# Six weight slots, a shared tile for the final norm's weights, and another order of pairs in a decoder trunk

## The chip, the cores and the metric

The kernel runs on one core of one Trainium2 chip. The metric is the device time of one execution in microseconds, as the median of several runs. Before the change it is 2187.33 us, the median of 3 runs from 2186.57 to 2188.96.

## What is computed

A two-layer decoder over 256 positions and 2048 channels, all in float32. Layer 0 mixes with a sliding-window attention beside an mLSTM, layer 1 with a forgetting attention; every layer is followed by a gated feed-forward part, and a norm ends the trunk:

```python
def swiglu(xn, w_gate, w_up, w_down):
    return (jax.nn.silu(xn @ w_gate) * (xn @ w_up)) @ w_down

    for layer in range(DEPTH):
        ...
        h = h + mix.astype(h.dtype)
        h = h + swiglu(rms_norm(h, norm_ffn[layer]), w_gate[layer], w_up[layer], w_down[layer])
    return rms_norm(h, norm_final)
```

The hidden width of the gated part is 5632. The weights, some 400 MB in all, are read once.

## The kernel before

**Three products for one.** To keep float32 precision with fast matmuls, every operand is split in two rounded parts, `hi` and `lo`, and a product is the sum of three matmuls: hi by hi, hi by lo, lo by hi (L164 to L166 in the projections, L345 to L347 in the gated part). Activations are split once (`xh`, `xl`, `mh`, `ml`). Weights are split as they stream in. `load_raw` (L85) has SyncE (SP) issue the load of a raw tile of 2 x 128 rows by 512 columns, 512 KB; the pool `wr` holds four such tiles. `split_chunk` (L138) lets ScalarE (ACT) round it to `hi` (L141) and VectorE (DVE) subtract to get `lo` (L142). The pool `wp` holds the `hi` and `lo` tiles, four slots of each. A raw slot comes free when VectorE has read it, a hi or lo slot when TensorE (PE) is through with it.

**The gated part.** `ffn` (L416) goes through the 11 groups of 512 hidden columns in two parts of 6 and 5 groups (`HALVES`). After the groups of a part comes a down projection over that part (L444 to L456). `gate_up` (L352) makes one group: it takes the 16 row blocks as 8 pairs, in the order of `ORDER` (L34), whose entries are (mixed or not, pair). For a plain pair it loads and splits one gate tile and one up tile and issues 2 x 2 x 2 x 3 = 24 matmuls. For a mixed pair, three of the eight, it computes the 2 x 2 block product of two row blocks of activations with gate and up with seven block products instead of eight, 21 matmuls. For that VectorE forms four combinations of the raw weights in the tile `t4` (L378 to L381; one buffer of 8 KB per partition), which are split in turn into `ht` and `lt` (L389, with the line of the helper L240 and L241 in the profile; two buffers each), and `lo` of one half tile (L384, also L241). The combinations of activations, `sh` and `sl`, come from `sums_of` (L199) while the output projection of the mixer writes its columns; `MIXED` names the pairs that have them. After the eight pairs VectorE adds the partial products up in the tile `c` (L405 to L413), ScalarE applies silu, VectorE multiplies (L430), and TensorE transposes `c` (L438) for the down projection.

**The end.** `finish` (L818) is called for each of the four column blocks of the last down projection. It adds to the residual `h`, squares, and multiplies by the final norm's weights `gf` (L827, for the last block L837). `gf` is 2048 floats on each of 128 partitions, 8 KB per partition, 1 MB to write. It has a tile of its own and is loaded by a DMA that GpSimd (POOL) issues (L813). Nothing precedes that load in its dependences, so it goes out at the start of the kernel. The power in L834 runs on POOL.

**The start.** SP loads the four column pieces of x and the first weights alternately (L96 to L99). TensorE transposes x piece by piece (L219) and multiplies with the key weights.

**Who orders the work.** The source is written in program order, and the Tile scheduler orders each engine's queue anew by a simulated timeline; within a queue an engine then works strictly in order. The number of slots and the order of pairs thus decide where an instruction stands in its queue.

**The scratch.** Some of each partition of the on-chip memory is set aside for the descriptors of POOL's DMAs. The program is made without a size for it, which gives 16 KB.

Of the kernel before, what the change touches and what calls it, by code (L numbers as in the profile page):

```python
# [7 lines left out]
F32 = mybir.dt.float32  # L8
# [7 lines left out]
P = 128  # L16
D = 2048
# [13 lines left out]
OFF_QM, OFF_KM, OFF_VM, OFF_OM = 1536, 2048, 2560, 3584  # L31
CAP = 15.0
FILL = 24
ORDER = ((0, 0), (0, 4), (1, 1), (0, 5), (1, 2), (0, 6), (1, 3), (0, 7))  # L34
MIXED = [p for w, p in ORDER if w]
HALVES = (0, 6, 11)

# [2 lines left out]
def trunk(  # L40
# [20 lines left out]
    nc = tc.nc  # L61
# [3 lines left out]
    xl = sp_.tile([P, KT, S], F32R, name="xl")  # L65
    mh = sp_.tile([P, KT, S], F32R, name="mh")
    ml = sp_.tile([P, KT, S], F32R, name="ml")
    wp = ctx.enter_context(tc.tile_pool(name="wp", bufs=4))
    wr = ctx.enter_context(tc.tile_pool(name="wr", bufs=4))
    cp = ctx.enter_context(tc.tile_pool(name="cp", bufs=1))  # L70
    sm = ctx.enter_context(tc.tile_pool(name="sm", bufs=2))
# [75 lines left out]
    def new_acc():  # L147
        return [pa.tile([P, NB], F32, tag="acc", name="acc") for _ in range(NT)]

    def gemm(acc, lhs, w, c0, n, k_from, k_to, k_all, skew=1):  # L150
        k0 = k_from
        while k0 < k_to:
            last = k_to == k_all and k0 + skew * CK >= k_all
            chunks = [load_chunk(w, kc, c0, n) for kc in range(k0, k_all if last else k0 + CK, CK)]
            order = [(i, t) for i in range(len(chunks) * CK) for t in range(NT)]
            if last:
                order.sort(key=lambda it: it[1])
            for i, t in order:
                k = k0 + i
                hi, lo = (c[:, i % CK, 0:n] for c in chunks[i // CK])  # L160
                ah, al = lhs(k)
                ts = slice(t * P, (t + 1) * P)
                o = acc[t][:, 0:n]
                nc.tensor.matmul(o, ah[:, ts], hi, start=(k == 0), stop=False)  # L164
                nc.tensor.matmul(o, ah[:, ts], lo, start=False, stop=False)  # L165
                nc.tensor.matmul(o, al[:, ts], hi, start=False, stop=(k == k_all - 1))  # L166
            k0 += len(chunks) * CK
# [4 lines left out]
    def m_of(k):  # L172
        return mh[:, k, :], ml[:, k, :]

    def project(w, c0, n):
        acc = new_acc()
        gemm(acc, x_of, w, c0, n, 0, KT, KT)
        return acc
# [3 lines left out]
    def square_sum(key, n):  # L182
        if n == 0:
            sums[key] = sm.tile([P, NT, 4], F32, tag="ss", name="ss")
        for t in range(NT):
            junk = sm.tile([P, NB], F32, tag="junk", name="junk")
            nc.scalar.activation(
                junk, h[:, t, n * NB : (n + 1) * NB], AF.Square, accum_out=sums[key][:, t, n : n + 1]
            )

    def rstd(key):
        tot = sm.tile([P, NT], F32, tag="tot", name="tot")
        nc.vector.reduce_sum(tot, sums[key], axis=AX)
        nc.vector.tensor_scalar(tot, tot, 1.0 / D, EPS, op0=ALU.mult, op1=ALU.add)
        r = sm.tile([P, NT], F32, tag="r", name="r")
        nc.gpsimd.tensor_tensor(out=r, in0=tot, in1=mhalf[:, 0:NT], op=ALU.pow)
        return r
# [41 lines left out]
    def split_plain(dst_h, dst_l, src):  # L239
        nc.scalar.copy(dst_h, src)  # L240
        nc.vector.tensor_tensor(out=dst_l, in0=src, in1=dst_h.bitcast(F32), op=ALU.subtract)  # L241

    def add_out(acc, n):
        for t in range(NT):
            o = h[:, t, n * NB : (n + 1) * NB]
            nc.vector.tensor_tensor(out=o, in0=acc[t], in1=o, op=ALU.add)
# [102 lines left out]
    def bank(par, name):  # L349
        return pm.tile([P, NB], F32, tag="pm", name=name) if par else pa.tile([P, NB], F32, tag="acc", name=name)  # L350

    def gate_up(fp, sh, sl, layer, g, par):  # L352
        c0 = g * NB
        plain = [[bank(par, "acc") for _ in range(NT)] for _ in range(2)]
        mixed = None
        count = [s_[0] for s_ in ORDER]
        for pos, (w, pair) in enumerate(ORDER):
            k0 = 2 * pair
            if not w:
                for m, wt in enumerate((w_gate[layer], w_up[layer])):  # L360
                    hi, lo = load_chunk(wt, k0, c0, NB)
                    for i in range(CK):
                        ah, al = x_of(k0 + i)
                        for t in range(NT):
                            ts = slice(t * P, (t + 1) * P)
                            three(
                                plain[m][t], ah[:, ts], al[:, ts], hi[:, i, :], lo[:, i, :],
                                pos == 0 and i == 0, pos == len(ORDER) - 1 and i == CK - 1,
                            )
# [46 lines left out]
    def ffn(layer, fp, sh, sl, eh, el, key, idx_next=None, key_next=None, finish=None):  # L416
        def a_of(k):
            return m_of(k) if k < KT else (eh[:, k - KT, :], el[:, k - KT, :])

        r = rstd(key)  # L420
        for part in range(2):
            g0, g1 = HALVES[part : part + 2]
            nk = 4 * (g1 - g0)
            for g in range(g0, g1):
                par = (g - g0 + part) % 2
                c = gate_up(fp, sh, sl, layer, g, par)
                for t in range(NT):
                    nc.scalar.activation(c[:, t, :], c[:, t, :], AF.Silu, scale=r[:, t : t + 1])
                for t in range(NT):
                    nc.vector.scalar_tensor_tensor(  # L430
                        out=c[:, t, :], in0=c[:, 2 + t, :], scalar=r[:, t : t + 1], in1=c[:, t, :], op0=ALU.mult, op1=ALU.mult
                    )
                for half in range(2):
                    pt = bank(par, "pf").rearrange("p (i q) -> p i q", i=2)
                    for i in range(2):
                        cs = (2 * half + i) * P
                        for t in range(NT):
                            nc.tensor.transpose(pt[:, i, t * P : (t + 1) * P], c[:, t, cs : cs + P], ident)  # L438
                    k = 4 * (g - g0) + 2 * half
                    if k < KT:  # L440
                        split_plain(mh[:, k : k + 2, :], ml[:, k : k + 2, :], pt)
                    else:
                        split_plain(eh[:, k - KT : k - KT + 2, :], el[:, k - KT : k - KT + 2, :], pt)
            wd = w_down[layer][4 * g0 * P : 4 * g1 * P, :]  # L444
            for n in range(4):
                acc = new_acc()
                end = part == 1 and idx_next is None and n == 3
                gemm(acc, a_of, wd, n * NB, NB, 0, nk, nk, skew=3 if end else 1)
                if part == 0:
                    add_out(acc, n)  # L450
                elif idx_next is None:
                    finish(acc, n)
                else:
                    add_out(acc, n)
                    split_scaled(idx_next, n)
                    square_sum(key_next, n)  # L456
# [20 lines left out]
    with tc.tile_pool(name="ev", bufs=1) as ev:  # L477
# [84 lines left out]
        acc = project(wi, OFF_OM + 768, 256 + 8)  # L562
# [53 lines left out]
        with tc.tile_pool(name="mp", bufs=1) as mp:  # L616
# [99 lines left out]
            for g in range(2):  # L716
                acc = project(wi, OFF_VM + g * NB, NB)
# [14 lines left out]
    with tc.tile_pool(name="od", bufs=1) as od:  # L732
# [8 lines left out]
        acc = project(wi1, c_v + 14 * FD, VT + FOX_H)  # L741
# [67 lines left out]
            )  # L809


    gf = cp.tile([P, D], F32, name="gf")
    nc.gpsimd.dma_start(gf, norm_final.partition_broadcast(P))  # L813
    ov = out[0].rearrange("(t p) d -> p t d", p=P)
    fs = cp.tile([P, NT, 4], F32, name="fs")
    ft = cp.tile([P, 3, NT], F32, name="ft")

    def finish(acc, n):  # L818
        ns = slice(n * NB, (n + 1) * NB)
        for t in range(NT):  # L820
            o = h[:, t, ns]
            nc.vector.tensor_tensor(out=o, in0=acc[t], in1=o, op=ALU.add)
            junk = sm.tile([P, NB], F32, tag="junk", name="junk")
            nc.scalar.activation(junk, o, AF.Square, accum_out=fs[:, t, n : n + 1])
            part, mean, rs = (ft[:, a, t : t + 1] for a in range(3))
            if n < 3:
                nc.vector.tensor_tensor(out=o, in0=o, in1=gf[:, ns], op=ALU.mult)  # L827
            if n == 2:
                nc.vector.reduce_sum(part, fs[:, t, 0:3], axis=AX)
                nc.vector.tensor_scalar(part, part, 1.0 / D, EPS, op0=ALU.mult, op1=ALU.add)  # L830
            if n < 3:
                continue
            nc.vector.tensor_scalar(mean, fs[:, t, 3:4], 1.0 / D, part, op0=ALU.mult, op1=ALU.add)
            nc.gpsimd.tensor_tensor(out=rs, in0=mean, in1=mhalf[:, 0:1], op=ALU.pow)  # L834
            nc.scalar.mul(h[:, t, 0 : 2 * NB], h[:, t, 0 : 2 * NB], rs)
            nc.vector.tensor_scalar(h[:, t, 2 * NB : 3 * NB], h[:, t, 2 * NB : 3 * NB], rs, None, op0=ALU.mult)
            nc.vector.scalar_tensor_tensor(out=o, in0=o, scalar=rs, in1=gf[:, ns], op0=ALU.mult, op1=ALU.mult)  # L837
            for half in (1, 0):
                hs = slice(half * 2 * NB, (half + 1) * 2 * NB)
                nc.sync.dma_start(ov[:, t, hs], h[:, t, hs])  # L840

    close_layer(1, w_out_odd[0], 3, "f1", finish=finish)


# [43 lines left out]
```

## Time and profile before

| | us |
|---|---|
| median of 3 runs | 2187.33 |
| lowest, highest | 2186.57, 2188.96 |
| the profiled execution | 2189.5 |
| its span in the profile | 2187.8 |
| matmuls busy in it | 2158.8 |
| VectorE busy | 1526.2 |
| ScalarE busy | 1118.1 |

The profile is of one execution. Its time is 1.7 us longer than the span from the first instruction to the last. Rows of a timeline name the start in microseconds from the start of the span, the busy time, the engine, the line, and out<-in by the names in the program; brackets at the end hold the idle time of the engine before it and who ended it. Rows of stretches show the busy time of each engine with the number of its instructions, the granted clock, the DMA share and GB/s. PEld is the loading of the stationary operand, which overlaps with matmuls. "q0" is the DMA queue of POOL, "q1" that of SP.

### The profile page before, as it was taken

To read this page: it belongs to the slowest core of one execution; us is meant where nothing else is said; L and a number is where in the kernel's file an instruction comes from. 1 tells how busy PE (TensorE), PEld (TensorE's weight loads), DVE (VectorE), ACT (ScalarE), POOL (GpSimd) and SP (SyncE) were. 2 spreads that over 40 slices of the span, in tenths; PEclk is the share of its full clock that TensorE was granted. 3 is DMA by queue.
4 is the path that set the end of the run, shared out by engine and by line. 5 is a ranking of instruction groups with operands and counts; after the bars stand their busy time and mean duration, and the time that the engine had idled before them with its cause. 6 is when DMAs were issued, how large, how long until landed. Compare 5 with 4: busy or idle time off the path is not lost.

```text
span 2187.8 us, 26662 instructions
## 1 busy us (share of the span) xinstructions
PE 2158.8 (99%) x9986; PEld 1782.2 (81%) x9986; DVE 1526.2 (70%) x1874; ACT 1118.1 (51%) x1447; POOL 37.6 (2%) x61
## 2 busy tenths in 40 slices
PE   8999999999999999999999999999999999999998
PEld 6878888877788888888888888888877888888886
DVE  5565567888874688885555555678888844888954
ACT  5565455555543455554545444555555533555543
POOL 2110000000000000000000000000000000000000
PEclk9999999999999999999999999999999999999999
DMA  8544556655666666565675565556565666666564
GB/s 257 149 148 148 171 167 185 198 178 189 202 196 193 191 200 204 174 212 185 182 224 168 169 175 156 181 182 194 190 203 173 212 193 193 195 200 200 189 198 144
DMA packets 213538, 408.34 MB, mean 187 GB/s; under 512 B 12736, under 2 KB 21024, under 8 KB 213152
## 3 DMA queue, kind: packets, MB, share of 16 engines
q1 hardware_dynamic: 212736, 402.90, 59.4%
q0 software_dynamic: 624, 3.72, 0.5%
q8 instruction: 78, 1.28, 0.2%
q14 instruction: 52, 0.43, 0.1%
q10 hardware_dynamic: 48, 0.02, 0.0%
HBM read 404.48 MB, written 2.11 MB: 186 GB/s over the span
## 4 chain that ended last, share of the span: by engine, by line
PE 65%; DVE 16%; DMA 13%; ACT 3%; issue 3%; SPq 0%; DVEq 0%; ACTq 0%; POOLq 0%; POOL 0%
PE acc L164 17%; PE acc L165 17%; PE acc L166 17%; DMA raw<-in_w_up_dram 9%; DVE lo L142 6%; DMA raw<-in_w_gate_dram 3%; PE acc L346 3%; PE acc L347 3%; PE acc L345 3%; DVE lt L241 2%; ACT hi L141 2%; DVE c L413 2%; DVE t L380 1%; DVE t L378 1%; PE prod L345 1%
## 5 line engine op out<-in xcount | busy, mean ns | idle before, releaser
L142 DVE TENSOR_TENSOR lo<-raw,hi 128x1024 fp32r<-128x1024 f32 (+3 forms) x710 | 851.2, 1202 | 490.2 <-ACT hi L141 488.1
L141 ACT CAST hi<-raw 128x1024 fp32r<-128x1024 f32 (+3 forms) x710 | 731.5, 1033 | 785.9 <-PE acc L166 498.0
L346 PE MATMUL acc<-lo,xh 128*128 128x512 f32 x946 | 369.9, 391 | 4.4 <-DVE lo L142 4.3
L347 PE MATMUL acc<-hi,xl 128*128 128x512 f32 x946 | 366.2, 390 | 0.0
L345 PE MATMUL acc<-hi,xh 128*128 128x512 f32 x946 | 349.8, 390 | 0.3 <-DVE c L407 0.3
L164 PE MATMUL acc<-hi,mh 128*128 128x512 f32 x768 | 299.9, 392 | 1.2 <-ACT mh L240 1.2
L165 PE MATMUL acc<-lo,mh 128*128 128x512 f32 x768 | 300.7, 392 | 0.0
L166 PE MATMUL acc<-hi,ml 128*128 128x512 f32 x768 | 298.4, 390 | 0.0
L165 PE MATMUL acc<-lo,xh 128*128 128x512 f32 (+3 forms) x736 | 276.0, 375 | 0.4 <-DVE lo L142 0.4
L164 PE MATMUL acc<-hi,xh 128*128 128x512 f32 (+3 forms) x736 | 275.1, 378 | 1.2 <-ACT hi L141 1.2
L166 PE MATMUL acc<-hi,xl 128*128 128x512 f32 (+3 forms) x736 | 276.2, 376 | 0.0
L346 PEld LDWEIGHTS acc<-lo,xh 128*128 128x128 f32 x946 | 177.6, 188 | 43.5 <-DVE lo L142 7.3
L345 PEld LDWEIGHTS acc<-hi,xh 128*128 128x128 f32 x946 | 177.6, 188 | 38.3 <-DVE c L407 0.8
L347 PEld LDWEIGHTS acc<-hi,xl 128*128 128x128 f32 x946 | 177.7, 188 | 36.3
L240 ACT CAST ht<-t 128x1024 fp32r<-128x1024 f32 x132 | 137.3, 1052 | 120.9 <-DVE t L381 59.4
L164 PEld LDWEIGHTS acc<-hi,mh 128*128 128x128 f32 x768 | 144.2, 188 | 31.2 <-ACT mh L240 1.4
L166 PEld LDWEIGHTS acc<-hi,ml 128*128 128x128 f32 x768 | 144.2, 188 | 29.6
L165 PEld LDWEIGHTS acc<-lo,mh 128*128 128x128 f32 x768 | 144.2, 188 | 29.2
L241 DVE TENSOR_TENSOR lt<-t,ht 128x1024 fp32r<-128x1024 f32 x132 | 158.2, 1217 | 2.9 <-ACT ht L240 2.7
L164 PEld LDWEIGHTS acc<-hi,xh 128*128 128x128 f32 x736 | 138.3, 189 | 26.4 <-issue 2.0
L165 PEld LDWEIGHTS acc<-lo,xh 128*128 128x128 f32 x736 | 139.1, 189 | 24.7 <-DVE lo L142 1.1
L166 PEld LDWEIGHTS acc<-hi,xl 128*128 128x128 f32 x736 | 139.1, 189 | 23.9 <-issue 0.3
(273 smaller groups left out, 2222.1 us busy)
## 6 DMA issues: line engine op xcount, KB each, us to landing
raw<-in_w_gate_dram SPq DMA_DIRECT2D x176, 512.0 KB, 4.0
raw<-in_w_up_dram SPq DMA_DIRECT2D x176, 512.0 KB, 4.6
raw<-in_w_down_dram SPq DMA_DIRECT2D x176, 512.0 KB, 3.7
raw<-in_w_in_odd_dram SPq DMA_DIRECT2D x88, 512.0 KB, 3.8
raw<-in_w_in_even_dram SPq DMA_DIRECT2D x64, 512.0 KB, 3.8
raw<-in_w_out_even_dram SPq DMA_DIRECT2D x32, 512.0 KB, 3.7
raw<-in_w_out_odd_dram SPq DMA_DIRECT2D x32, 512.0 KB, 3.7
raw<-in_w_in_odd_dram SPq DMA_DIRECT2D x8, 272.0 KB, 2.8
```

Source lines behind the costliest of these rows:

```text
L141: nc.scalar.copy(hi[:, :, 0:n], raw[:, :, 0:n])
L142: nc.vector.tensor_tensor(out=lo[:, :, 0:n], in0=raw[:, :, 0:n], in1=hi[:, :, 0:n].bitcast(F32), op=ALU.subtract)
L164: nc.tensor.matmul(o, ah[:, ts], hi, start=(k == 0), stop=False)
L165: nc.tensor.matmul(o, ah[:, ts], lo, start=False, stop=False)
L166: nc.tensor.matmul(o, al[:, ts], hi, start=False, stop=(k == k_all - 1))
L240: nc.scalar.copy(dst_h, src)
L241: nc.vector.tensor_tensor(out=dst_l, in0=src, in1=dst_h.bitcast(F32), op=ALU.subtract)
L345: nc.tensor.matmul(o, ah, hi, start=start, stop=False)
L346: nc.tensor.matmul(o, ah, lo, start=False, stop=False)
L347: nc.tensor.matmul(o, al, hi, start=False, stop=stop)
L378: nc.vector.tensor_tensor(out=t4[:, 0, :], in0=ru[:, 0, :], in1=rg[:, 0, :], op=ALU.subtract)
L413: nc.vector.tensor_tensor(out=o, in0=plain[m][t], in1=o, op=ALU.add)
```

## The change

The hi and lo pool gets six slots of each instead of four, 16 KB more per partition. To make room, `gf` loses its own tile: its load is written after the groups of the last part, into the buffer of `t4` (same tag, one buffer), whose last contents are read by then; and the DMA scratch is given 8 KB instead of 16. The order of pairs becomes 0 1 2 4 3 5 6 7, with 2, 3 and 6 mixed, where it was 0 4 1 5 2 6 3 7 with 1, 2 and 3 mixed. The pattern of plain and mixed places is the same.

```diff
-ORDER = ((0, 0), (0, 4), (1, 1), (0, 5), (1, 2), (0, 6), (1, 3), (0, 7))
+ORDER = ((0, 0), (0, 1), (1, 2), (0, 4), (1, 3), (0, 5), (1, 6), (0, 7))
...
-    wp = ctx.enter_context(tc.tile_pool(name="wp", bufs=4))
+    wp = ctx.enter_context(tc.tile_pool(name="wp", bufs=6))
...
+            gf = None
+            if part == 1 and finish is not None:
+                gf = fp.tile([P, D], F32, tag="t4", name="gf", bufs=1)
+                nc.gpsimd.dma_start(gf, norm_final.partition_broadcast(P))
             wd = w_down[layer][4 * g0 * P : 4 * g1 * P, :]
             for n in range(4):
                 acc = new_acc()
...
-                    finish(acc, n)
+                    finish(acc, n, gf)
...
-    gf = cp.tile([P, D], F32, name="gf")
-    nc.gpsimd.dma_start(gf, norm_final.partition_broadcast(P))
...
-    def finish(acc, n):
+    def finish(acc, n, gf):
...
-    nc = _bacc.Bacc("TRN2", target_bir_lowering=False, num_devices=1)
+    nc = _bacc.Bacc("TRN2", target_bir_lowering=False, num_devices=1, dynamic_dma_scratch_size=8192)
```

## The prediction

> **What bounds the kernel now.** I read the page first, then the waits of TensorE, then the busy time by stretches, then the timeline of one group of the gated layer. The page:
>
> ```profile
> span 2187.8 us, 26662 instructions
> PE 2158.8 (99%) x9986; PEld 1782.2 (81%) x9986; DVE 1526.2 (70%) x1874; ACT 1118.1 (51%) x1447; POOL 37.6 (2%) x61
> PE 65%; DVE 16%; DMA 13%; ACT 3%; issue 3%; SPq 0%; DVEq 0%; ACTq 0%; POOLq 0%; POOL 0%
> ```
>
> Matmuls are busy 99% of the span, but only 65% of the chain that ended last is PE; DVE and DMA hold 29% of it. The busy share can mislead: a matmul's end is modelled, so a late one shows little idle time. The weight loads (PEld) have no such tail, and there is one for each matmul, so their share of a stretch tells its pace. Here are the gated stretches between the first and the last group of each part, one per row, and last a down projection:
>
> ```profile
> core 0: us, PE busy (x) PEld busy (x) DVE busy (x) ACT busy (x) POOL busy (x), PEclk, DMA share, GB/s
> 426.29:603.40 177.11, 172.90 (x765) 139.70 (x764) 153.59 (x185) 94.35 (x108) 0.00 (x0) 1.00 0.61 190
> 822.61:948.50 125.89, 125.11 (x558) 101.94 (x557) 109.62 (x132) 68.81 (x79) 0.00 (x0) 1.00 0.62 194
> 1496.57:1711.50 214.93, 211.12 (x938) 171.29 (x937) 185.81 (x223) 117.02 (x134) 0.00 (x0) 1.00 0.60 193
> 1888.70:2055.90 167.20, 166.88 (x750) 137.25 (x749) 148.60 (x178) 93.05 (x107) 0.00 (x0) 1.00 0.62 199
> 615.00:780.00 165.00, 165.00 (x733) 136.65 (x732) 98.90 (x100) 71.76 (x72) 0.00 (x0) 1.00 0.63 197
> ```
>
> In the down projection, which never waits, weight loads fill 136.65 / 165.00 = 82.8%. At that share the four gated stretches would need 168.7, 123.1, 206.8 and 165.7 us. They took 8.4, 2.8, 8.1 and 1.5 us more: **20.8 us** lost over 16 group periods. So TensorE sets the time, and some 1% of it is waiting inside the gated groups, most in the first part of each layer. The Trainium skill's Perfetto Trace Analysis, section Identifying the Most-Contended Engine, says that matmul busy share misjudges the distance to the bound and that weight-load share is the better measure; by its 81% alone one would look for 19%, and the row of the down projection shows that 82.8% is full pace here.
>
> Who is late is in the timeline of one group (VectorE first, then TensorE, then ScalarE):
>
> ```profile
> 1589.26 2.59 DVE L142 TENSOR_TENSOR lo<-raw,hi 128x1024 fp32r<-128x1024 f32 x2 [1.38 <-ACT hi L141]
> 1591.76 0.68 DVE L406 TENSOR_TENSOR u<-prod,c 128x512 f32<-128x512 f32 x1
> 1595.35 0.69 DVE L378 TENSOR_TENSOR t<-raw 128x512 f32<-128x512 f32 x1 [2.91 <-DMA raw<-in_w_up_dram]
> 1595.96 0.68 DVE L379 TENSOR_TENSOR t<-raw 128x512 f32<-128x512 f32 x1
> ...
> 1598.95 1.22 DVE L142 TENSOR_TENSOR lo<-raw,hi 128x1024 fp32r<-128x1024 f32 x1
> 1600.09 0.68 DVE L409 TENSOR_TENSOR c<-prod,c 128x512 f32<-128x512 f32 x1
> ```
> ```profile
> 1598.99 0.39 PE L345 MATMUL acc<-hi,xh 128*128 128x512 f32 x1
> 1600.22 0.50 PE L346 MATMUL acc<-lo,xh 128*128 128x512 f32 x1 [0.85 <-DVE lo L142]
> ```
> ```profile
> 1592.61 1.05 ACT L141 CAST hi<-raw 128x1024 fp32r<-128x1024 f32 x1 [2.03 <-PE acc L347]
> ```
> ```profile
> 1590.51 4.72 DMA raw<-in_w_up_dram
> ```
>
> At a group's end VectorE combines its four products (from L406 on, which must wait for the last mixed matmul). Straight behind L406 stands the first combination of the next group's mixed pair (L378), whose raw tile was only asked for at 1590.51, when the lo before L406 had freed the slot; it takes 4.72 us. VectorE idles 2.91 us, everything behind it is late, and TensorE's matmul of 1598.99 is followed by the next at 1600.22, a whole us late. ScalarE meanwhile waits 2.03 us for one of the four hi slots. VectorE has no lead over TensorE to absorb this.
>
> **The change part by part.**
>
> *Six slots of hi and lo.* No operation is added; the scheduler rewrites the queues. A group uses 16 raw tiles and, with one pair being multiplied, four slots let VectorE stand one pair ahead, six let it stand two. In the built order of the changed kernel, within a steady group, L378 to L381 of that first mixed pair no longer stand behind L406 but 4.7 us of VectorE work ahead of it; behind L406 come one lt and the combination itself. I add VectorE's own work (1.14 us for a 1024-wide operation, 0.60 for a 512-wide one: the starts at 1598.95 and 1600.09, 1595.35 and 1595.96) between the last read of a raw slot and the first use of its next content. For the mixed pair's two tiles it was 2.88 and 1.74 us, and becomes 5.70 and 4.56. Loading takes:
>
> ```profile
> raw<-in_w_gate_dram SPq DMA_DIRECT2D x176, 512.0 KB, 4.0
> raw<-in_w_up_dram SPq DMA_DIRECT2D x176, 512.0 KB, 4.6
> ```
>
> So the shortest cover, 1.74 us against 4.6, was 2.9 us short, the 2.91 of the timeline; 4.56 is not. From L406 to the tile that TensorE then needs most urgently there were 11.8 us of VectorE work beside 13.8 us of matmuls, too little for a wait of 2.9; now it is 1.7 us beside 6.8. What is late next: the raw ring, still four tiles, and the ht/lt buffers, still two. One steady group:
>
> ```profile
> 1579.50:1623.90 44.40, 43.21 (x193) 34.96 (x192) 38.34 (x47) 23.97 (x29) 0.00 (x0) 1.00 0.59 190
> ```
> ```profile
> L141 ACT CAST hi<-raw 128x1024 fp32r<-128x1024 f32 (+3 forms) x710 | 731.5, 1033 | 785.9 <-PE acc L166 498.0
> ```
>
> Full pace is 34.96 / 0.828 = 42.2 us; VectorE needs 38.3 us of it, so it can afford 3.9 us of waiting per group. In the new order three covers ahead of plain lo tiles are 4.08 us against 4.6 + 1.03 (landing, then ScalarE's cast): 1.6 us each, 4.7 in all if every one is met while VectorE is needed. That is near the edge, so I don't take the whole 20.8 us. The best stretch of the trace, the last row of the four, loses 1.5 us in 4 periods, 0.37 each; at that rate 16 periods still lose 5.9, and the gain is 20.8 - 5.9 = **14.9 us**. Ends: 0 (VectorE's loop stays the bound) and 20.8.
>
> *gf in the dead t4 tile.* At the start of the kernel, gf's 1 MB leaves. Rows of TensorE, and of the DMA queues from 10 to 15 us:
>
> ```profile
> 13.88 0.61 PE L166 MATMUL acc<-hi,xl 128*128 128x512 f32 x2
> ...
> 16.54 0.41 PE L219 MATMUL pt<-ident,h 128*128 128x128 f32 x2 [2.04 <-DMA h<-in_x_dram]
> ```
> ```profile
> DMA packets 586, 2.08 MB, mean 416 GB/s; under 512 B 42, under 2 KB 45, under 8 KB 469
> q0 software_dynamic: 265, 1.46, 70.1%
> q1 hardware_dynamic: 321, 0.62, 33.0%
> ```
> ```profile
> 6.41 0.54 POOL L813 DMA_DIRECT2D gf<-in_norm_final_dram  x1
> ```
>
> While TensorE waits for the third piece of x, POOL's queue (gain's 0.5 MB and gf's 1 MB) holds 70% of the DMA engines. Without gf, x lands 1.05 MB / 416 GB/s = 2.5 us earlier, and the 2.04 us wait goes: **-2.0 us** (ends 0 and -2.5), and it stays gone, since later stages are dense. POOL's queue is 0.54 us shorter there.
>
> At the end gf is issued once t4's last reader is through, with the weights of the last down projection on the other queue:
>
> ```profile
> 2060.93 2.36 DVE L241 TENSOR_TENSOR lt<-t,ht 128x1024 fp32r<-128x1024 f32 x2
> 2099.13 1.28 DVE L827 TENSOR_TENSOR h<-h,gf 128x512 f32<-128x512 f32 x2
> ```
> ```profile
> cb<-scratch POOLq DMA_DIRECT2D x1, 2048.0 KB, 10.8
> ```
>
> The last reader ends at 2063.3, the first user starts at 2099.1: 36 us for a transfer of half the size of cb's, which took 10.8. Behind the wait on POOL stand only the two powers of the end (L834). It costs the weights: at q0's 292 GB/s (1.46 MB in 5 us) gf takes 3.6 us, in which q1 gets 124 GB/s instead of the 197 that the down projection draws: 0.26 MB, 1.3 us of supply, partly covered by the tiles ahead. I take **+1.0** (ends 0 and 2.5, a full stop for 1 MB). The Trainium skill's SBUF — State Buffer, Summary: rules for kernel authors, advises against hiding a POOL-issued DMA under VectorE, whose double-rate operations starve descriptor writing; by that gf would come later than 10 us, and the sum would stay as it is below 36. The trace has cb landing in 10.8 us with VectorE at work.
>
> *8 KB of scratch*: no time of its own; at worst POOL waits at the start with its next DMA, ahead of work (the selects, L531's biases) that nothing needs before the first attention. 0. *The order of pairs* keeps the pattern of plain and mixed, so the matmul count stays; only each layer's first group asks for other pairs. Pair 6's sums move to the last output column, some 2 us of VectorE, and in the built order stand 10 us of matmuls ahead of their use. 0, ends ±2. The rest of TensorE's queue (attention, mLSTM) keeps its places within 8 matmuls, but for one small transpose at the start: 0, ends ±2.
>
> Sum: -14.9 - 2.0 + 1.0 = **-15.9 us**. The profiled execution took 2189.5 us with its span of 2187.8; it lies 2.2 us over the median 2187.33. Taken from the median: **2171.4 us** (-0.73%).
>
> **The rivals.**
>
> *The raw ring takes the slots' place, mildly.* All three short covers are met: 38.3 + 4.7 = 43.0 us per group, 0.8 over full pace. 16 periods then lose 12.8 us instead of 20.8, a gain of 8.0; with the rest -9.0: about 2178. For it: the DMA waits in VectorE's chain. Against: VectorE's lead absorbs single waits.
>
> *It takes their place wholly: slower.* Once VectorE's waits pass 3.9 us a group, they set the period. With loads at the longest wait of this group's chain,
>
> ```profile
> 1582.76 5.34 DMA raw<-in_w_up_dram
> ```
>
> a cover is short 5.34 + 1.03 - 4.08 = 2.3 us, three make 6.9, the period 45.2, 3.0 over full pace; 16 lose 48 us instead of 20.8: +27 us, with the rest about 2213. For it: VectorE running ahead asks for raw tiles in tighter pairs. Against: queue use stays at 60%.
>
> *Nothing in the groups*: the scheduler's new order waits elsewhere for as long; only the start gains: -1, about 2186.
>
> *All goes*, the 20.8 and 2 us more: about 2165.
>
> **How the numbers follow.** Forecast (2167 to 2175) 0.55; raw ring mildly 0.17; nothing 0.10; slower 0.12; all goes 0.06. A measurement of this kernel tells about 0.2% (4.4 us) from no change. Faster by more: 0.55 + 0.17 + 0.06 = 0.78; within: 0.10; slower: 0.12. For 8 in 10 the range takes the forecast, the mild ring, most of "all goes" and what lies between: 2165 to 2184.
>
> **What would show it.** In the changed trace: weight loads near 82.8% in the gated stretches (81% or more in the first parts, where 78.9 and 79.7% stand now); L378's waits for raw of 2 to 3 us behind L406 gone, ScalarE's waits for TensorE's slots short; no 2 us gap of TensorE at 14 us; gf's landing well ahead of L827. Wrong, if VectorE's idle time before L142 by raw tiles grows past 3.9 us a group with TensorE still waiting for lo and lt, or if the down projection after the last group shows waits for raw.

## The result and the profile after

The changed kernel takes 2179.09 us, the median of 5 runs (2177.11 to 2179.37); the kernel before, run beside it, takes 2188.94 (5 runs, 2186.57 to 2192.2). The ratio is 0.9954 with a 95% interval of 0.9939 to 0.9968: **9.85 us or 0.46% faster**, where 15.9 us were forecast. Run once more later, the same kernel took 2174.34 us against 2188.09, a ratio of 0.9938 (0.9926 to 0.9951), 13.75 us faster. The two intervals overlap; by the medians the gain is 10 to 14 us.

The page after (its profiled execution took 2177.11 us):

```profile
span 2175.4 us, 26701 instructions
PE 2152.4 (99%) x9986; PEld 1783.4 (82%) x9986; DVE 1526.5 (70%) x1874; ACT 1118.8 (51%) x1447; POOL 37.7 (2%) x61
```

The busy times are those of before to within 0.4% on every engine: the change does no work less. The span is 12.4 us shorter, more than the medians differ by, since the changed kernel's profiled execution was the shortest of its five. The gated stretches of the changed kernel, first to last group of each part, and the down projection below them, columns as before:

```profile
422.46:595.63 173.17, 172.44 (x774) 141.82 (x773) 154.37 (x185) 96.09 (x110) 0.00 (x0) 1.00 0.61 197
809.05:939.53 130.48, 129.51 (x582) 106.54 (x580) 115.43 (x138) 71.79 (x82) 0.00 (x0) 1.00 0.60 196
1486.16:1700.42 214.26, 211.20 (x948) 173.81 (x947) 188.38 (x225) 117.98 (x134) 0.00 (x0) 1.00 0.59 191
1875.27:2045.40 170.13, 168.17 (x756) 138.59 (x755) 149.71 (x180) 92.76 (x106) 0.00 (x0) 1.00 0.59 191
606.63:771.63 165.00, 165.00 (x733) 136.68 (x732) 98.36 (x99) 72.39 (x73) 0.00 (x0) 1.00 0.62 197
```

The down projection still loads weights 82.8% of the time. With the full pace of the prediction's last row (136.65 / 165.00, unrounded), each gated stretch loses its length less PEld divided by that share: 1.9, 1.8, 4.4 and 2.8 us, **10.9 us** where before lost 20.8. In the profiled execution of the second timing the same sum is 7.9. So 9.9 to 12.9 us of the lost time came back, and 8 to 11 did not. The waits of TensorE tell what most of the rest is (engine, line, tile and who released it: us in all, times, longest):

```profile
PE acc L345 <- DVE u L406: 6.6, 9, 1.6
PE pg L128 <- DMA gn<-in_norm_mix_dram: 3.9, 1, 3.9
PE pt L219 <- DMA h<-in_x_dram: 1.3, 2, 1.1
```

The first row is new. Before, TensorE waited inside the groups for `lo`:

```profile
PE acc L346 <- DVE lo L142: 4.3, 6, 1.0
PE acc L346 <- DVE lo L241: 3.1, 11, 0.3
```

These waits are gone. Now the first matmul on a plain accumulator waits for L406, which writes nothing that TensorE reads. What L406 gives it is a **bank of PSUM**. A group's plain products stand in one pool of four banks and its mixed products in the other (`bank`, L349), and the pools change places from group to group; so the next group's plain accumulators take the four banks that the mixed products leave. L406 is the only reader of `mixed[3]`. Around the second longest of these waits, VectorE, then the chain of waits in the same stretch (start, length, what), then TensorE:

```profile
1966.91 1.22 DVE L142 TENSOR_TENSOR lo<-raw,hi 128x1024 fp32r<-128x1024 f32 x1 [0.19 <-ACT hi L141]
1968.68 0.69 DVE L378 TENSOR_TENSOR t<-raw 128x512 f32<-128x512 f32 x1 [0.55 <-DMA raw<-in_w_up_dram]
1969.29 0.69 DVE L379 TENSOR_TENSOR t<-raw 128x512 f32<-128x512 f32 x1
1969.89 0.68 DVE L380 TENSOR_TENSOR t<-raw,t 128x512 f32<-128x512 f32 x1
1970.49 1.22 DVE L142 TENSOR_TENSOR lo<-raw,hi 128x1024 fp32r<-128x1024 f32 x1
1971.63 0.68 DVE L381 TENSOR_TENSOR t<-raw,t 128x512 f32<-128x512 f32 x1
1972.23 1.22 DVE L241 TENSOR_TENSOR lt<-t,ht 128x1024 fp32r<-128x1024 f32 x1
1973.36 0.68 DVE L406 TENSOR_TENSOR u<-prod,c 128x512 f32<-128x512 f32 x1
```
```profile
1962.62 5.93 DMA raw<-in_w_up_dram
```
```profile
1968.48 0.39 PE L347 MATMUL prod<-ht,sl 128*128 128x512 f32 x1
...
1972.33 0.39 PE L347 MATMUL acc<-hi,xl 128*128 128x512 f32 x1
1974.10 0.50 PE L345 MATMUL acc<-hi,xh 128*128 128x512 f32 x1 [1.38 <-DVE u L406]
```

The last mixed product was done at 1968.9. L406 could have run then, but it starts at 1973.36: VectorE works its queue in order, and the next group's L378 to `lt`, 4.68 us, stand in front of it. Besides, L378 had itself waited 0.55 us for a raw tile that took 5.93 us. TensorE runs out of free banks and starts 1.77 us after the matmul before, where 0.23 is the rule in these rows. That is 1.54 us late for a wait shown as 1.38; so the nine waits stand for some 8 of the 10.9 us, and no row of waits names the others.

At the start of the kernel the 2 us gap is gone: the transpose follows at once.

```profile
13.78 0.62 PE L166 MATMUL acc<-hi,xl 128*128 128x512 f32 x2
14.25 0.38 PE L219 MATMUL pt<-ident,h 128*128 128x128 f32 x2
```

### The profile page after: what moved, and what is told of

The parts are those of the page before. It is cut to its first block, busy times and chain, and to the rows that moved or that the text cites. A ratio compares the mean times of both kernels' runs of the same rounds, so it can differ in the third digit from the quotient of the medians.

```text
span 2175.4 us, 26701 instructions
## 1 busy us (share of the span) xinstructions
PE 2152.4 (99%) x9986; PEld 1783.4 (82%) x9986; DVE 1526.5 (70%) x1874; ACT 1118.8 (51%) x1447; POOL 37.7 (2%) x61
## 4 chain that ended last, share of the span: by engine, by line
PE 76%; DVE 13%; DMA 7%; issue 2%; ACT 1%; DVEq 0%; SPq 0%; ACTq 0%; POOLq 0%; POOL 0%
PE acc L166 17%; PE acc L165 17%; PE acc L164 17%; DMA raw<-in_w_up_dram 6%; PE acc L345 6%; PE acc L346 6%; PE acc L347 6%; DVE lo L142 4%; DVE lt L241 2%; PE prod L345 1%; PE prod L347 1%; PE prod L346 1%; DVE t L378 1%; DVE t L380 1%; DVE t L381 1%
## 5 line engine op out<-in xcount | busy, mean ns | idle before, releaser
L345 PE MATMUL acc<-hi,xh 128*128 128x512 f32 x946 | 368.0, 391 | 6.7 <-DVE u L406 6.6
```

Of the source, the lines that this page charges most:

```text
L345: nc.tensor.matmul(o, ah, hi, start=start, stop=False)
```

## The experiments

**The first theory** (T1 below): the look-ahead that the slots allow stands in front of L406 in VectorE's queue, the bank of `mixed[3]` is handed over late, and this alone takes the rest of the gain. **Its rival** (T2): the loop of raw tiles between VectorE and the DMA queue still sets the pace, and L406 is only the place where it shows. A third (T3) asks for the share of the pair order. Each kernel was timed beside the kernel before; "lost" is the gated stretches' lost time as above, from the kernel's own profile, and the bank wait is what TensorE's rows of waits give in all for the readers of mixed products.

| slots, raw tiles, other | median us | against before | ratio (95%) | lost, us | bank wait, us |
|---|---|---|---|---|---|
| before: 4, 4 | 2188 to 2191 | | | 20.8 | 0.3 |
| changed: 6, 4 | 2179.09 | -9.9 | 0.9954 (0.9939 to 0.9968) | 10.9 | 6.6 |
| changed, second time | 2174.34 | -13.8 | 0.9938 (0.9926 to 0.9951) | 7.9 | 4.1 |
| 6, 4, L378 behind L406 | 2174.98 | -15.1 | 0.9931 (0.9918 to 0.9943) | 4.8 | none |
| 6, 4, copy | 2168.19 | -21.9 | 0.9901 (0.9888 to 0.9915) | 2.8 | none |
| 6, 4, old order | 2175.73 | -14.4 | 0.9936 (0.9923 to 0.9948) | 12.9 | 8.8 |
| 6, 4, old order, copy | 2168.20 | -23.1 | 0.9897 (0.9882 to 0.9912) | 1.6 | none |
| 4, 4 | 2182.28 | -7.8 | 0.9968 (0.9956 to 0.9980) | 14.4 | none |
| 4, 4, old order | 2187.18 | -4.1 | 0.9983 (0.9974 to 0.9991) | 21.6 | 0.7 |
| 4, 4, copy | 2194.39 | +3.1 | 1.0016 (1.0006 to 1.0025) | 27.9 | 7.4 |
| 5, 4 | 2196.40 | +5.1 | 1.0022 (1.0011 to 1.0033) | 23.5 | 19.1 |
| 5, 4, copy | 2184.78 | -3.3 | 0.9982 (0.9973 to 0.9991) | 20.2 | 8.1 |
| 5, 6 | 2166.08 | -22.0 | 0.9907 (0.9892 to 0.9922) | 0.2 | none |
| 5, 6, copy | 2166.56 | -21.5 | 0.9904 (0.9890 to 0.9917) | 0.1 | none |

Take the lost time from the median, and 2163 to 2173 us are left in every row: most of what the kernels differ in, 2166 to 2196 us, is lost in the gated groups.

**L406 first.** An edge in the issue order alone:

```diff
-            nc.vector.tensor_tensor(out=t4[:, 0, :], in0=ru[:, 0, :], in1=rg[:, 0, :], op=ALU.subtract)
+            with tc.issue_after(combined[0]) if first and g not in HALVES else nullcontext():
+                nc.vector.tensor_tensor(out=t4[:, 0, :], in0=ru[:, 0, :], in1=rg[:, 0, :], op=ALU.subtract)
...
-        nc.vector.tensor_tensor(out=u2, in0=mixed[3], in1=c[:, 0, :], op=ALU.add)
+        u2_add = nc.vector.tensor_tensor(out=u2, in0=mixed[3], in1=c[:, 0, :], op=ALU.add)
+        combined[0] = u2_add.ins
```

> The changed kernel with one edge in the issue order: the first combination (L378) of a group's first mixed pair is queued on VectorE behind the u2 addition (L406) of the group before. Nothing is added or left out. T1 (the new waits of TensorE for L406, 6.6 us, come from VectorE's queue: the run-ahead block stands in front of L406 and TensorE's next plain accumulator waits for the bank that L406 hands over): the waits named L406 fall below 3 us and the kernel gains 3 to 6 us more, so 12.5 to 16 us under the kernel before. T2 (the loop of raw tiles between VectorE and the DMA queue sets the pace and L406's lateness is only where it shows): the waits move to lo and lt, VectorE waits longer for raw tiles, and the kernel stays at 8 to 11 us under the kernel before, or loses part of it.

No wait names this addition any more, and 4.8 us are lost instead of 10.9 or 7.9; the gain is 15.1 us. The scheduler also ordered the first layer's mixer anew: the first group's combination starts at 386.8 us, where the changed kernel has 383.8, so 3 us of the gain went there. T1's number was met. T2's signs are absent: no wait inside the groups names `lo` or `lt`, and VectorE's combinations waited 19.3 us in all for raw tiles, no longer than before the edit. But the second timing of the changed kernel gained 13.8, only 1.3 us less, and the two intervals overlap: what speaks for T1 here are the waits and the lost time, not the median alone.

**The bank freed by ScalarE.** VectorE's queue nearly as it was, the bank read out by another engine:

```diff
-        nc.vector.tensor_tensor(out=u2, in0=mixed[3], in1=c[:, 0, :], op=ALU.add)
+        nc.scalar.copy(u2, mixed[3])
+        nc.vector.tensor_tensor(out=u2, in0=u2, in1=c[:, 0, :], op=ALU.add)
```

> The changed kernel with mixed[3] copied out of its bank by ScalarE, so that u2 is added from SBUF: one 128x512 ScalarE copy more per group (22 in all, about 0.6 us each by ScalarE's other copies), VectorE's queue stands as it did. T1: the bank comes free without VectorE, the waits of TensorE for L406 (6.6 us) vanish, and the kernel stands 12.5 to 16 us under the kernel before. T2: no gain, 8 to 11 us under. If the copy comes late in ScalarE's own queue, the waits stay and carry its name.

With six slots the gain grows to 21.9 us, past the 12.5 to 16 of T1; the wait for the bank is gone, and only 2.8 us are lost, though 22 ScalarE copies were added. The raw ring is the same four tiles, and VectorE waited for L378's tile as long as in the changed kernel:

```profile
DVE t L378 <- DMA raw<-in_w_up_dram: 24.1, 25, 3.0
```
```profile
DVE t L378 <- DMA raw<-in_w_up_dram: 21.3, 24, 2.4
```

(the kernel with the copy, then the changed kernel). So T2 as it stood has fallen: with six slots the handing over of the bank costs time that the raw waits alone don't.

**Four slots, and the order of pairs.** The changed kernel with `bufs=4` for the pool `wp`; with the old `ORDER` and six slots; with both; and with the old `ORDER`, six slots and ScalarE's copy.

> The changed kernel with four slots again; the new pair order, gf in the t4 buffer and the smaller scratch stay. If the slots alone carry the gated stretches (T1 and T2 both say so): only the start's 2.3 us and what the attention layers gained remain, 1.5 to 4 us under the kernel before. T3 (the pair order carries part of it): 5 us or more under.

> The changed kernel with the pair order of before (0 4 1 5 2 6 3 7, mixed 1 2 3); six slots, gf and scratch as changed. T1 and T2: the built order of VectorE around L406 is the same with either pair order, so it stands where the changed kernel does, 8 to 12 us under the kernel before. T3: it differs from the changed kernel by 3 us or more to one side.

> The changed kernel with four slots and the pair order of before: only gf's move and the smaller scratch are left. The built order of VectorE around L406 is that of the kernel before. If the pair order made the 7.8 us that the run with four slots gained: 1 to 4 us under the kernel before, the start's share alone. If gf's move made it: 6 us or more under.

> Six slots, ScalarE's copy of mixed[3], and the pair order of before. With the bank free in time the pair order should not matter with six slots: within 3 us of the run with the copy and the new order, 18.5 to 25 us under the kernel before. If the new order carries some of that: 12 to 18 us under.

Four slots with the new order gain 7.8 us, where T1 and T2 had 1.5 to 4. With both put back the gain is 4.1 (by the interval 2.0 to 5.7), which is what moving gf and halving the scratch are worth together. So with four slots the new order seems to be worth some 4 us: 14.4 us lost instead of 21.6, though the two intervals overlap a little. With six slots no worth is seen: the old order has 0.9936, past the 8 to 12 us that T1 and T2 gave it, but the changed kernel has 0.9954 and 0.9938, and with the copy the two orders agree to 0.01 us in the medians, as expected. T3 holds, if at all, only where slots are few. Beyond gf, the slots gain about 10 us with the old order (14.4 - 4.1), and 2 to 6 us with the new one.

**The copy with four slots**, the same edit with `bufs=4`, was meant as a control in which nothing is to be freed.

> A control: ScalarE's copy of mixed[3], but with four slots (new pair order, gf moved). T1: with four slots the run-ahead block does not stand in front of L406 and no TensorE wait names it, so there is nothing for the copy to free: within 2.5 us of the run with four slots, 5 to 10.5 us under the kernel before. Rival: the copy helps by itself, whatever the slots (an add from SBUF that is shorter, a bank that is free sooner in every group): 12 us or more under.

It took 10.9 us more against before than four slots without the copy, which neither expectation had. Its VectorE and TensorE:

```profile
1589.85 0.68 DVE L407 TENSOR_TENSOR u<-u,c 128x512 f32<-128x512 f32 x1
1594.49 0.69 DVE L378 TENSOR_TENSOR t<-raw 128x512 f32<-128x512 f32 x1 [3.95 <-DMA raw<-in_w_up_dram]
1595.10 0.68 DVE L379 TENSOR_TENSOR t<-raw 128x512 f32<-128x512 f32 x1
1595.70 0.68 DVE L408 TENSOR_TENSOR c<-prod,u 128x512 f32<-128x512 f32 x1
```
```profile
1596.44 0.50 PE L345 MATMUL acc<-hi,xh 128*128 128x512 f32 x1 [2.16 <-DVE c L408]
```

The addition after the copied one (L408 here, reading `mixed[2]`) stands behind an L378 that waits 3.95 us for its raw tile, and TensorE waits for that bank. It is the same hand-over, one bank later; and what makes it late here is less the work in front of it than a **wait** in front of it. Why the raw tile came later than without the copy was not followed.

**Five slots.** `bufs=5`, nothing else.

> Five slots in place of six, all else as changed. In the built order 1.8 us of the next group's run-ahead (L378 to L380) stand in front of L406 instead of 4.7. T1: the waits for L406 fall below 4 us and the kernel is at least as fast as the changed one, 9 to 15 us under the kernel before. T2: fewer tiles ahead of TensorE, more waits for lo and lt, 6 to 9 us under.

Both expectations were plainly wrong: 5.1 us slower than before, with the longest bank waits of all. The rows of waits of TensorE and of VectorE, then a stretch of VectorE's timeline and the matmul behind it:

```profile
PE acc L345 <- DVE u L406: 19.1, 8, 3.7
```
```profile
DVE t L378 <- DMA raw<-in_w_up_dram: 56.4, 37, 3.9
```
```profile
2027.13 0.69 DVE L378 TENSOR_TENSOR t<-raw 128x512 f32<-128x512 f32 x1 [2.10 <-DMA raw<-in_w_up_dram]
2027.74 0.68 DVE L379 TENSOR_TENSOR t<-raw 128x512 f32<-128x512 f32 x1
2028.34 1.22 DVE L142 TENSOR_TENSOR lo<-raw,hi 128x1024 fp32r<-128x1024 f32 x1
2029.47 0.68 DVE L380 TENSOR_TENSOR t<-raw,t 128x512 f32<-128x512 f32 x1
2030.08 1.22 DVE L241 TENSOR_TENSOR lt<-t,ht 128x1024 fp32r<-128x1024 f32 x1
2031.21 0.68 DVE L406 TENSOR_TENSOR u<-prod,c 128x512 f32<-128x512 f32 x1
```
```profile
2031.95 0.79 PE L345 MATMUL acc<-hi,xh 128*128 128x512 f32 x1 [3.31 <-DVE u L406]
```

The mistake was to count work only, and in one group: 1.8 us of work stood ahead of L406 there, 4.1 in the group shown. L378 waits for its raw tile 56 us in all, over twice as long as with six slots, and each such wait delays L406 as well. T1's cause, work ahead of L406, is only a part of it.

**Five slots with the copy, and five slots with six raw tiles** (`bufs=6` for `wr`; the memory of six slots and four raw tiles), without and with the copy.

> Five slots with ScalarE's copy of mixed[3]. With five slots TensorE waited 19.1 us for L406, because VectorE's L378 stood in front of it and itself waited 56 us for raw tiles. T1 (the bank is the cost): 13 to 19 us under the run with five slots, so 8 to 15 us under the kernel before; a rest is possible in which the next bank (mixed[2], freed by the following addition) stands behind the same L378. T2 (the raw tiles are the cost, the bank only the place where it shows): the same loss comes back as waits for lo and lt, and it stays within 4 us of the run with five slots.

> Five slots and six raw tiles in place of four (the SBUF of six slots and four raw tiles), no copy. If L406 is late because L378 in front of it waits for its raw tile: VectorE's waits of 56 us for L378's tile fall under 20, TensorE's waits for L406 from 19.1 to under 9, and it stands 8 to 14 us under the kernel before. If VectorE's work in front of L406 is enough to make it late: the raw waits fall, the waits for L406 stay over 12 us, and it stands within 4 us of the kernel before.

> Five slots, six raw tiles and ScalarE's copy of mixed[3]. T1: the bank was the last thing in TensorE's way, so the ring of raw tiles adds nothing to six slots with the copy: 18 to 24 us under the kernel before, no L406 wait. T2 (the ring still holds part of the pace): 25 us or more under.

The copy gives back 8.4 us of five slots' time, less than T1 expected and more than T2. Waits of TensorE for the copied bank stay, 7.7 of the 8.1 us in the table, and the profile shows why (ScalarE, then TensorE):

```profile
916.80 1.04 ACT L240 CAST ht<-t 128x1024 fp32r<-128x1024 f32 x1 [3.14 <-DVE t L379]
917.76 0.58 ACT L406 COPY u<-prod 128x512 f32<-128x512 f32 x1
```
```profile
918.39 0.50 PE L345 MATMUL acc<-hi,xh 128*128 128x512 f32 x1 [2.19 <-ACT u L406]
```

On ScalarE too the hand-over stands behind a cast that waits for L379, thus for the same raw tile. With six raw tiles the whole thing is gone, copy or not. TensorE's waits in the kernel with five slots, six raw tiles and no copy, complete but for the one that starts the kernel (4.2 us for the gains):

```profile
PE acc L164 <- ACT mh L240: 1.2, 1, 1.2
PE pt L219 <- DMA h<-in_x_dram: 0.8, 1, 0.8
PE acc L164 <- ACT hi L141: 0.7, 1, 0.7
```
```profile
419.41:588.94 169.53, 169.53 (x765) 140.34 (x764) 152.17 (x182) 96.98 (x108) 0.00 (x0) 1.00 0.63 201
...
1480.04:1688.04 208.00, 208.00 (x939) 172.24 (x938) 186.74 (x223) 119.39 (x135) 0.00 (x0) 1.00 0.63 197
```

Nothing is left inside the groups: 140.34 / 169.53 is 82.8%, the pace of the down projection, and TensorE is busy all the time. The 22 us are far past the 8 to 14 that were expected. L378 still waits for raw tiles 26 us in all, where under 20 were expected:

```profile
DVE t L378 <- DMA raw<-in_w_up_dram: 26.2, 21, 2.5
```

But no matmul is late by it, and that with two or more operations of the look-ahead, L378 among them, still in front of L406 in all but the last group of a part. So neither the place in the queue nor a wait for a raw tile costs anything by itself; the cost comes when the look-ahead is held up so long that L406 runs after TensorE needs the bank. T2 is right in that with five slots more raw tiles cure everything; T1 in that the bank is where TensorE pays, and that a copy out of it in time cures nearly as much with four raw tiles and six slots. The 25 us or more that T2 expected of both cures together did not come: there was nothing left to gain.

**The changed kernel again.**

> The changed kernel once more, unedited, to stand beside the others: 8 to 12 us under the kernel before.

13.8 us, a little past the upper end; 7.9 us lost instead of 10.9 and 4.1 us of bank waits instead of 6.6. The same program thus loses more in one execution than in another; why was not followed.

What was not tried: the halved scratch alone, gf alone, and six slots with more than four raw tiles.

## Why the prediction was right, and where it was not

**Right:** TensorE sets the time and the loss sits in the gated groups at the pace of 82.8%; the slots take VectorE's look-ahead past it; the waits for `lo` went; the first parts now load weights 141.82 / 173.17 = 81.9% and 173.81 / 214.26 = 81.1% of the time, as the prediction asked. One of its signs came by half: ScalarE's waits for a slot that a gated matmul still held fell from 129.7 to 83.9 us, not to little. The Trainium skill's Perfetto Trace Analysis, Identifying the Most-Contended Engine, which advised weight-load share over matmul busy share, is borne out: 99% busy on the page stood for 20.8, 10.9 and 0.2 us lost alike.

The first median, 2179.09 us, lies past the forecast's own band of 2167 to 2175; the second, 2174.34, lies inside it. The wide range holds both. In the profiled executions 9.9 us for the groups and 3.3 for the start, with nothing for gf, make 13.2, where the spans differ by 12.4.

**The start, -2.0:** the gap is gone, and the first combination of the changed kernel starts 3.3 us earlier (383.8 for 387.1). In the kernel with four slots and the old order, which shares with it only gf and the scratch, it is 1.8 (385.4). The term holds. **gf at the end, +1.0:** too high. The view of its tile in the changed kernel (instructions, with first and last start; then its landing):

```profile
L829 DVE TENSOR_TENSOR h<-h,gf x6: 681/682/683, 2087.2 to 2142.2; 128x512 f32<-128x512 f32 x6
...
L447 POOL DMA_DIRECT2D gf<-in_norm_final_dram x1: 587/587/587, 2054.2 to 2054.2; - x1
...
DMA to landing us min/median/max: 8.3/8.3/8.3
```

It landed 25 us ahead of its first user, and TensorE has no wait in that time: weight loads fill 33.98 of the 41.00 us from 2046 to 2087, 82.9%. The Trainium skill's SBUF — State Buffer, Summary: rules for kernel authors, warns of a POOL-issued DMA beside VectorE operations at double rate. VectorE was busy 8.6 of the 9 us from 2054, and this 1 MB landed in 8.3 us; whether an operation there ran at double rate no row tells. The prediction's comparison with cb says less than it seems: its 10.8 us were for 2 MB, and VectorE was busy only 4.9 of the 11 us from 1102.

**The order, 0:** not told from 0 with six slots; with four it seems to be worth some 4 us, outside the ±2 that was given.

**The step that failed is the gated groups' term, 14.9 us.** It measured 9.9 us in the first profiled execution and 12.9 in the second. Three links of it did not hold.

- The residual was taken as 0.37 us a period, the rate of the best old stretch. It is 8 to 11 us over 16 periods, 0.5 to 0.7. That rate belonged to a queue in which L406 stood ahead of L378; the change turned these two around, and the prediction said so.
- It then asked only what stands *behind* L406 ("one lt and the combination itself") and for which tile TensorE would wait. It did not ask who waits for L406. Its 4.7 us of VectorE work ahead of L406 is 4.68 in the timeline above, but was booked as look-ahead gained, not as a bank held back.
- "4.56 is not" short: it still was at times. L378's waits fell from 39 to 24 and from 52.3 us in all (the row of before stands below) to 21.3, but a tile that took 5.93 us kept it waiting 0.55 us, and L406 behind it.

```profile
DVE t L378 <- DMA raw<-in_w_up_dram: 52.3, 39, 2.9
```

The rival of the mild raw ring gave 2178 us, 1 us from the first median. Its cause is shown for five slots, where two more raw tiles take 23.5 us lost down to 0.2; for six slots, the changed kernel, no run shows how much of the 8 to 11 us is the ring's. And it priced the wrong place, so its nearness in number is luck. It had VectorE's period pass TensorE's by three short covers ahead of `lo`; no wait of TensorE names `lo`, the longest names a bank. "All goes", 2165 us, came not with this change but with five slots and six raw tiles: 2166.08.

The Trainium skill's Perfetto Trace Analysis says in Optimization Strategy that the same gap repeating on the engine that should be saturated can mean too little SBUF or PSUM for the next tile. The runs agree: TensorE waited 6.6 us in all for a PSUM bank to come free, and with five slots two more raw tiles in SBUF ended such waits.

## What to carry to other kernels

When more buffers let an engine run ahead, look in its queue for what the look-ahead now stands in front of, and for who waits for *that*: an addition that hands back a PSUM bank is urgent for TensorE even if its result is not. Deepen the buffer whose arrival the first instruction of the look-ahead waits for before the one behind it: here the same memory gave 10 to 14 us as six weight slots with four raw tiles, and 22 us as five and six. And try the sizes between: five slots with four raw tiles were slower than four and than six.

## What the runs showed that was not expected

- With the rest of the change in place, four slots were 7.8 us faster than the kernel before, five 5.1 us slower and six 10 to 14 us faster. The time does not follow the number of buffers in one direction where a scheduler orders the queues anew for each.
- 22 ScalarE copies more (0.58 us each in the timeline) cost no measurable time with six slots and gained 8 us or more: ScalarE was 51% busy, and the place in its queue counted, not the work.
- The same program lost 10.9 us in one profiled execution and 7.9 in another, with medians 4.75 us apart. Differences of 4 us between kernels that were not run side by side, the worth of the pair order with four slots among them, are therefore not shown here.
